# Two-layer encoder on one core: heads cross in pairs, merged rows turned in two chunks, pool products two projections later, another MLP entry

## The chip, the cores and the metric

The kernel runs on one core of one Trainium2 chip. The metric is the device time of one execution in microseconds (us), the median of several runs. TensorE (PE in the profile, PEld its weight loads) multiplies matrices, VectorE (DVE) and ScalarE (ACT) work element by element, GpSimd (POOL) does little here, and SyncE (SP) issues the DMAs. SBUF is the on-chip memory of 128 partitions, PSUM holds matmul results.

## The reference, cut to what matters

Two layers on x (1, 256, 1024), float32. Each layer is a token mixer and a gated MLP, both with RMSNorm ahead and a residual add behind.

```python
def _token_mixer(xn, w_in, w_pool, pool_scale, w_a, w_b, w_o, rel_bias):
    u, q, k, v, g_pool, g_attn = jnp.split(xn @ w_in, SPLITS, axis=-1)
    pooled = ...   # centred means of u over 2, 4, 8, 16 tokens, minus u, by 4 channel groups
    pool_out = jnp.einsum('bsgc,gcd->bsgd', pooled, w_pool).reshape(B, S, POOL_WIDTH) * pool_scale
    # 12 heads of 128 in 3 groups (window, dilation): (128,1), (512,4), (2048,16); softmax with a bias;
    # heads of the same number in the 3 groups are combined by their softmax denominators: 4 heads come out
    merged = jax.nn.sigmoid(g_pool) * (pool_out @ w_a) + jax.nn.sigmoid(g_attn) * (attn_out @ w_b)
    return merged @ w_o

def _conv_ffn(xn, w_up, conv_w, conv_b, w_down):     # D_FF = 2816 = 22 chunks of 128
    a, gval = jnp.split(xn @ w_up, 2, axis=-1)
    a = conv3(a, conv_w) + conv_b                    # depthwise along the tokens
    return (jax.nn.gelu(a) * gval) @ w_down
```

## The kernel before, in words

**Number format.** To keep float32 accuracy at TensorE's faster rate, operands are split into a high part (cast to float32r) and a low part (the difference). A product is three matmuls: high by high, high by low, low by high. Activations are split once; weights are split on the way.

**Weights.** Class `Weights` (L82 to L202) streams all weights in an order written out at L236 to L278. A raw load of 1 MB (L118, on SP's queue, three buffers `raw`) is cut into two pieces; ACT casts each to `wh` (L178) and DVE subtracts to get `wl` (L179). Five pairs wh/wl can be live, and splitting runs up to three pieces ahead of use.

**Order of a layer.** The work is written out in one stream, and a scheduler places the instructions on the engines: first values v from the normed rows; then u and the pool means; 24 projections `proj` (L491, 16 matmuls each) for q and k, in the order of `PAIRS`; then 8 pieces of `by_rows` (L589, 12 matmuls each) for the pool gate and pool_out @ w_a; 12 pieces for the attention gate and attn_out @ w_b; the output projection `residual_mm` (L518), whose last four of eight k are held back so that the first results come out early; then the MLP.

**Attention, by visits.** The last 12 projections and the 8 pieces each call `step` (L975) once: 20 visits, numbered from 0. `VISITS` (L40) gives, for heads 0 to 3, the visit of each of four functions: `scores` (L897: logits, softmax in `probs`), `turn` (L927), `parts` (L943) and `weigh` (L953). `turn` transposes the probabilities in 32 by 32 blocks on DVE (L931) into `rows`, a single buffer, and starts `cross` (L601): sixteen DMAs within SBUF of 32 partitions each (L606, on SP's queue), four per visit, that bring the blocks to their partitions in `pt`. `parts` splits the first group's probabilities into `pth` (ACT, L948) and `ptl` (DVE, L949), both from a pool tag with two buffers. `weigh` multiplies them with the values: `o_ps`, six matmuls by pth and ptl (L958) and four by pt (L962); ACT and DVE bring the result into `at2` (L967, L968).

**Pool products.** `pool_out` (L867) is a generator of four parts of twelve matmuls (L479 to L481) into `pool_ps`, split into `po` (L880, L881); one part runs after each of projections 4 to 7 (m == 1).

**Merged rows.** The gated sum must be turned for the output projection. Its first 512 channels (`way`) go through a block transpose (L1058) and `cross` under the work of the next pieces (`merged_parts`, L1036). The other 512 (`th`, `turned`, L1062 to L1072) come last and are turned by `blocks` (L609): sixteen DVE transposes (L614), each of four 32 by 32 blocks for the two token halves; then in two halves ACT casts (L1071) and DVE subtracts (L1072) into `m`.

**MLP entry.** For the first four chunks of D_FF (`ENTRY`, 512 columns of a) the projection is taken by rows (L1102 to L1129) as soon as the first tokens are normed; the rows `a_rows` are then turned by sixteen PE transposes `a_turn` (L1114) and copied by DVE (L1116) into `a_first`. `up(f)` (L1131) takes chunk by chunk: a and g projections, convolution, gelu, product; `residual_mm` for w_down follows `LAG` = 6 chunks behind.

Of the kernel before, what the change touches and what calls it, by code (L numbers as in the profile page):

```python
# [10 lines left out]
F32 = mybir.dt.float32  # L11
# [5 lines left out]
P = 128  # L17
# [19 lines left out]
WARM = (5, 1, 2, 1)  # L37
PAIRS = (2, 4, 0, 1, 3, 5)
LAG = 6
VISITS = ((0, 3, 12, 13), (1, 5, 13, 17), (6, 10, 18, 22), (7, 11, 19, 23))  # L40
ENTRY = 4
HALVES = (slice(0, 512), slice(512, D))
SEGMENTS = (HALVES, (slice(0, 512), slice(512, 768), slice(768, D)))

# [161 lines left out]
def encoder(ctx, tc, x, w_in, w_pool, pool_scale, w_a, w_b, w_o, norm1, norm2, w_up, conv_w,  # L206
# [29 lines left out]
    for l in range(DEPTH):  # L236
        for g in range(NG):
            c0 = C_V + g * 512
            slots = (("m2", 0, 2), ("m2", 1, 2), ("ybig",), ("at2",)) if g == 0 else ()
            for j in range(2):  # L240
                tag = "k1" if l == 0 and g == 1 and j == 0 else None
                W.use(rows(w_in[l], j * 512, 4, c0, 512, tag), slots[2 * j : 2 * j + 2])
        if l == 0:
            W.n_scaled = len(W.pieces)
        for c in range(3, -1, -1):
            W.use(cols(w_in[l], c * 256))
        for n, c in enumerate(PAIRS):
            pool = ([], [])
            if n == 1:
                pool = W.add(  # L250
                    w_pool[l].rearrange("g (k p) c -> p (g k) c", p=P), (8, 256),
                    [((lambda t, j=j: t[:, 4 * j : 4 * j + 4, :]), (4, 256)) for j in range(2)],
                )
                pool = (pool[:1], pool[1:])
            for j, c0 in enumerate((C_Q, C_K)):
                a, b = cols(w_in[l], c0 + c * 256)
                W.use([a] + pool[j] + [b])
        for w, c0 in ((w_in[l], C_GP), (w_a[l], 0)):
            for half in HALVES:
                for j in range(2):  # L260
                    W.use(rows(w, j * 512, 4, c0 + half.start, 512))
        for half in HALVES:
            for j in range(2):
                W.use(rows(w_in[l], j * 512, 4, C_GA + half.start, 512))
            W.use(rows(w_b[l], 0, 4, half.start, 512))
        for c in range(4):
            W.use(rows(w_o[l], c * 256))
        slots = (("v1",), ("ybig",), ("at2",))
        for j in range(2):
            W.use(rows(w_up[l], j * 512, 4, 0, 512), slots[2 * j : 2 * j + 2])  # L270
        for f in range(0, NF, 2):
            a = cols(w_up[l], f * P) if f >= ENTRY else []
            g = cols(w_up[l], DFF + f * P)
            W.use([a[0], g[0], a[1], g[1]] if a else g)
            if f >= LAG:
                W.use(rows(w_down[l], (f - LAG) * P))
        for f in range(NF - LAG, NF, 2):
            W.use(rows(w_down[l], f * P))  # L278
# [3 lines left out]
    xv = x[0].rearrange("(m t) d -> m t d", t=2)  # L282

    def gain(src):
        g = sm.tile([P, D], F32, tag="gain", bufs=1, name="gain")
        nc.sync.dma_start(out=g, in_=src.partition_broadcast(P))
        return g

# [61 lines left out]
    def load_bias():  # L350
        oh = big.tile([P, NT * 256], F32, tag="ybig", name="onehot_sb")
        nc.gpsimd.memset(oh, 0.0)
        rb = sm.tile([P, P], F32, tag="s", name="rb")
        nc.gpsimd.memset(rb, 0.0)
        for r in (0, 64):
            nc.sync.dma_start(out=oh[r : r + 33, :], in_=onehot)
            for g in range(NG):
                cc = slice(32 * g, 32 * g + HPG)
                nc.sync.dma_start(out=rb[r : r + 32, cc], in_=rel_bias[:, g * HPG : (g + 1) * HPG])
        for g in range(NG):  # L360
            nc.gpsimd.memset(rb[32:33, 32 * g : 32 * g + HPG], 1.0)
        rr = big.tile([P, P], F32R, tag="at2", name="rr")
        nc.vector.tensor_copy(rr, rb)
        nc.vector.tensor_sub(
            out=rr[64:96], in0=rb[64:96], in1=rr[64:96].bitcast(F32)
        )
        ohr = big.tile([P, NT * 256], F32R, tag="m2", name="onehot_r")
        nc.scalar.copy(out=ohr, in_=oh)
        return rr, ohr
# [239 lines left out]
    def blocks(out, in_):  # L609

        for i in range(4):
            for j in range(4):
                a, b = slice(32 * i, 32 * i + 32), slice(32 * j, 32 * j + 32)
                nc.vector.transpose(out=out[b, :, :, a], in_=in_[a, :, :, b])  # L614

    def two_parts(tag, name):

# [163 lines left out]
    for l in range(DEPTH):  # L781
# [43 lines left out]


        plh = big.tile([P, KD, 2, P], F32R, tag="ybig", name="plh")
        pll = big.tile([P, KD, 2, P], F32R, tag="xn", name="pll")
        pooled = {}
        for gi in range(3, -1, -1):  # L830
            w = WINDOWS[gi]
# [63 lines left out]
        probs, ptiles, crossing = {}, {}, []  # L895

        def scores(hh):  # L897
            probs[hh] = sm.tile([P, 2, 512], F32, tag="s", name="probs")
# [28 lines left out]

        def turn(hh):

            rows = sm.tile([P, 4, 2, 4, 32], F32, tag="gain", bufs=1, name="rows")  # L930
            nc.vector.transpose(  # L931
                out=rows.rearrange("p j t c r -> p (t c) j r"),
                in_=probs[hh].rearrange("p t (c j r) -> p (t c) j r", c=4, j=4),
            )
            if hh % 2 == 0:
                ptiles["pair"] = big.tile(
                    [P, 2, 4, 2, 4, 32], F32, tag=("ybig", "xn")[hh // 2], name="pt"
                )
            ptiles[hh] = ptiles["pair"][:, hh % 2]
            crossing.append(cross(ptiles[hh], rows))  # L940

        def parts(hh):
            pt = ptiles[hh].rearrange("p i t c r -> p c t i r")  # L943
            pth = sm.tile([P, 2, 2, P], F32R, tag="us", name="pth")
            ptl = sm.tile([P, 2, 2, P], F32R, tag="us", name="ptl")
            for c in range(2):
                hi, lo = (a[:, c].rearrange("p t (i r) -> p t i r", i=4) for a in (pth, ptl))
                nc.scalar.copy(out=hi, in_=pt[:, c])  # L948
                nc.vector.tensor_sub(out=lo, in0=pt[:, c], in1=hi.bitcast(F32))  # L949
            ptiles[hh] = pth, ptl, pt[:, 2:4]  # L950

        def weigh(hh):
            pth, ptl, pt = ptiles[hh]  # L953
            ps = acc.tile([P, 2, P], F32, tag="acc", name="o_ps")
            for kc in range(2):
                c = slice(hh * P, (hh + 1) * P)
# [16 lines left out]
                visits[visit].append((f, hh))  # L973

        def step():  # L975
            for f, hh in visits.pop(0):
                f(hh)
            if crossing and next(crossing[0], "end") == "end":
                crossing.pop(0)


        for m, c in enumerate(PAIRS):
            if m == 1:
                po2 = two_parts("m2", "po2")
                pool_parts = pool_out(po2)
            if m == 2:

                qkl = big.tile([P, 2, HPG, 2, P], F32R, tag="xn", name="qkl")
                ql, kl = qkl[:, 0], qkl[:, 1]
            for n in range(4):  # L990
                src, rest = (halves(a) for a in proj(x2))
                if m == 1:
# [52 lines left out]
        for n, cc in enumerate(HALVES):  # L1045
# [17 lines left out]
            else:  # L1063
                assert next(first, None) is None
                turned = big.tile([P, 4, 2, P], F32, tag="v0", name="turned")
                blocks(
                    turned.rearrange("p c t q -> p t c q"), th.rearrange("p t (c k) -> p t c k", c=4)
                )
                for k in range(0, 4, 2):
                    hi, lo = (a[:, 4 + k : 6 + k] for a in (mh, ml))  # L1070
                    nc.scalar.copy(out=hi, in_=turned[:, k : k + 2])  # L1071
                    nc.vector.tensor_sub(out=lo, in0=turned[:, k : k + 2], in1=hi.bitcast(F32))  # L1072
# [26 lines left out]
        acts = {}  # L1099


        a_first = big.tile([P, ENTRY, S], F32, tag="gates", name="a_first")  # L1102

        rows_of_a = big.tile([P, 2, ENTRY * P], F32, tag="m2", name="a_rows")

        def keep_entry(t, ps):
            r = rows_of_a[:, t]
            nc.scalar.copy(out=r, in_=ps)
            return r

        def turn_entry(t, r):
            pt = mmp.tile([P, ENTRY, P], F32, tag="mm", name="a_turn")
            for f in range(ENTRY):
                nc.tensor.transpose(pt[:, f, :], r[:, f * P : (f + 1) * P], ident)  # L1114
            av = a_first.rearrange("p f (m t) -> p f m t", t=2)[:, :, :, t]
            nc.vector.tensor_copy(av, pt)  # L1116

        held, ps = entry
        first = keep_entry(0, ps)
        ps = v_tile()  # L1120
        for n in range(4):
            v_sum(ps, x2, 1, n, held[n])
            if n == 1:
                turn_entry(0, first)
        for i, _ in held:
            W.free(i)
        last = keep_entry(1, ps)
        g_first = [proj(x2)]
        turn_entry(1, last)  # L1129

        def up(f):  # L1131
            w0, w1, w2, b = (prm[:, l, j * NF + f : j * NF + f + 1] for j in range(4))
            if f < ENTRY:
                a = a_first[:, f, :]
# [92 lines left out]
```

## Time and profile before

| | us |
|---|---|
| runs | 889.36, 888.7, 886.91; median 888.7 |
| profiled execution | 886.12 |
| its span | 884.3 (granted TensorE clock 0.999) |
| TensorE busy | 864.0 (98%) |
| VectorE busy | 674.0 (76%) |
| ScalarE busy | 498.2 (56%) |

The profile records one execution. Its span runs from the first to the last instruction; the rest of the execution's time, 1.8 us, lies around it. Times in a timeline count from the span's start. A line number is that of the kernel's source, but a helper has one line for all its callers, so the tile names tell them apart. A matmul's recorded duration is longer than its pitch, since matmuls overlap: 128x256 shows 0.28 us and follows at 0.12, 128x512 shows 0.39 and follows at 0.23.

### The profile page before, as it was taken

The page shows a single profiled execution, that of the slowest core. Times are in us where ns is not written, and L with a number is a line of the kernel's source. Part 1 is how long each engine was busy: PE and PEld are TensorE (multiplying, and loading weights), DVE is VectorE, ACT ScalarE, POOL GpSimd, SP SyncE. Part 2 cuts the span into 40 slices and gives each one's busy share as a digit, 9 for nine tenths or more (in the row PEclk, how much of TensorE's full clock was granted, in tenths as well). Part 3 has the DMA queues.
Part 4 walks back from the last instruction along what each step waited for, and adds up shares of the span by engine and source line. Part 5 has one row for each costly group of instructions (what it writes and reads, how often), then busy time and mean ns, then how long its engine had stood idle before and what let it go on. Part 6 is the DMA issues. An engine that isn't in the chain of part 4 may idle for free.

```text
span 884.3 us, 12329 instructions
## 1 busy us (share of the span) xinstructions
PE 864.0 (98%) x4554; PEld 739.7 (84%) x4554; DVE 674.0 (76%) x1088; ACT 498.2 (56%) x817; POOL 15.6 (2%) x45
## 2 busy tenths in 40 slices
PE   9999999999899999999999999999998999999997
PEld 7888988788788888888888898887886888888886
DVE  7997795656788987787856968774559798878774
ACT  7745554534448766666545565454444586656653
POOL 2000000000010000000000000000000100000000
PEclk9999999999999999999999999999999999999999
DMA  9668736376464565465626465455745547556541
GB/s 330 215 233 264 254 127 211 122 278 191 167 211 147 203 224 191 160 221 191 238 96 232 149 199 183 140 196 161 251 151 203 195 157 246 183 190 199 182 143 49
DMA packets 121480, 169.86 MB, mean 192 GB/s; under 512 B 5814, under 2 KB 89478, under 8 KB 121292
## 3 DMA queue, kind: packets, MB, share of 16 engines
q1 hardware_dynamic: 121404, 169.07, 57.0%
q8 instruction: 36, 0.59, 0.3%
q14 instruction: 24, 0.20, 0.1%
q10 hardware_dynamic: 16, 0.00, 0.0%
HBM read 162.74 MB, written 3.69 MB: 188 GB/s over the span
## 4 chain that ended last, share of the span: by engine, by line
PE 79%; DVE 7%; DMA 6%; SPq 5%; issue 1%; ACT 1%; POOLq 0%; DVEq 0%; ACTq 0%; POOL 0%
PE proj_ps L487 25%; PE proj_ps L489 13%; PE rows_ps L584 10%; PE v_ps L584 6%; PE res_ps L515 5%; PE res_ps L516 5%; PE res_ps L514 5%; SPq L606 5%; DMA raw<-in_w_in_dram 4%; PE v_ps L773 2%; DVE wl L179 2%; DVE turned L614 2%; PE v_ps L686 1%; ACT wh L178 1%; PE o_ps L962 1%
## 5 line engine op out<-in xcount | busy, mean ns | idle before, releaser
L179 DVE TENSOR_TENSOR wl<-raw,wh 128x1024 fp32r<-128x1024 f32 x274 | 333.8, 1223 | 143.5 <-ACT wh L178 139.3
L178 ACT CAST wh<-raw 128x1024 fp32r<-128x1024 f32 x274 | 286.5, 1050 | 213.4 <-PE proj_ps L487 69.6
L487 PE MATMUL proj_ps<-x,wh 128*128 128x512 f32 x1152 | 288.8, 392 | 0.0
L487 PEld LDWEIGHTS proj_ps<-x,wh 128*128 128x128 f32 x1152 | 208.2, 189 | 38.0
L489 PEld LDWEIGHTS proj_ps<-x,wl 128*128 128x128 f32 x1152 | 157.2, 190 | 11.3
L489 PE MATMUL proj_ps<-x,wl 128*128 128x256 f32 x1152 | 160.8, 282 | 0.0
L584 PE MATMUL rows_ps<-wh,x 128*128 128x512 f32 x256 | 81.7, 392 | 0.0
L514 PE MATMUL res_ps<-wh,actq 128*128 128x512 f32 (+1 forms) x184 | 70.2, 381 | 0.0
L515 PE MATMUL res_ps<-wl,actq 128*128 128x512 f32 (+1 forms) x184 | 70.1, 381 | 0.0
L516 PE MATMUL res_ps<-wh,actk 128*128 128x512 f32 (+1 forms) x184 | 69.9, 380 | 0.0
L584 PEld LDWEIGHTS rows_ps<-wh,x 128*128 128x128 f32 x256 | 48.1, 188 | 9.7
L584 PE MATMUL rows_ps<-wl,x 128*128 128x512 f32 x128 | 49.8, 389 | 0.0
L584 PE MATMUL rows_ps<-wh,po 128*128 128x512 f32 x128 | 40.3, 391 | 0.0
L516 PEld LDWEIGHTS res_ps<-wh,actk 128*128 128x128 f32 x184 | 34.6, 188 | 6.7
L514 PEld LDWEIGHTS res_ps<-wh,actq 128*128 128x128 f32 x184 | 34.7, 188 | 6.2
L515 PEld LDWEIGHTS res_ps<-wl,actq 128*128 128x128 f32 x184 | 34.7, 188 | 6.0
L514 PE MATMUL res_ps<-wh,m 128*128 128x512 f32 (+1 forms) x72 | 26.8, 372 | 5.6 <-ACT m L1042 5.6
L1157 ACT ACTIVATE y<-y 128x256 f32<-128x256 f32 x44 | 18.3, 416 | 24.1 <-DVE y L1154 24.0
L1140 ACT ACTIVATE y<-a,prm 128x256 f32<-128x256 f32 x36 | 21.6, 599 | 16.0 <-DVE a L510 16.0
L584 PEld LDWEIGHTS rows_ps<-wh,po 128*128 128x128 f32 x128 | 24.0, 188 | 4.9
L584 PEld LDWEIGHTS rows_ps<-wl,x 128*128 128x128 f32 x128 | 24.1, 188 | 4.7
L515 PE MATMUL res_ps<-wl,m 128*128 128x512 f32 (+1 forms) x72 | 26.8, 373 | 1.0 <-DVE wl L179 1.0
(208 smaller groups left out, 1135.2 us busy)
## 6 DMA issues: line engine op xcount, KB each, us to landing
raw<-in_w_in_dram SPq DMA_DIRECT2D x58, 1024.0 KB
raw<-in_w_up_dram SPq DMA_DIRECT2D x44, 1024.0 KB
raw<-in_w_down_dram SPq DMA_DIRECT2D x22, 1024.0 KB
raw<-in_w_a_dram SPq DMA_DIRECT2D x8, 1024.0 KB
raw<-in_w_o_dram SPq DMA_DIRECT2D x8, 1024.0 KB
pt<-rows SPq DMA_DIRECT2D x128, 32.0 KB
raw<-in_w_b_dram SPq DMA_DIRECT2D x4, 1024.0 KB
sk<-fd SPq DMA_DIRECT2D x1, 2560.0 KB
```

The lines of the kernel that those rows point to most:

```text
L178: lambda: nc.scalar.copy(out=h, in_=src),
L179: lambda: nc.vector.tensor_sub(out=l, in0=src, in1=h.bitcast(F32)),
L487: nc.tensor.matmul(ps, wh(k), x2[:, k], start=(k == 0), stop=False)
L489: nc.tensor.matmul(ps[:, 1], wl(k), x2[:, k, 0], start=False, stop=(k == nk - 1))
L514: nc.tensor.matmul(ps, ah, wh, start=first, stop=False)
L515: nc.tensor.matmul(ps, ah, wl, start=False, stop=False)
L516: nc.tensor.matmul(ps, al, wh, start=False, stop=last)
L584: nc.tensor.matmul(ps, x2[:, 2 * n + j, part, t, :], w[:, j, :], start=(n + m == 0), stop=(n == of - 1 and m == 5),)
L606: nc.sync.dma_start(out=out[b, i], in_=in_[a, j])
L614: nc.vector.transpose(out=out[b, :, :, a], in_=in_[a, :, :, b])
L1140: nc.scalar.activation(y, a, AF.Identity, bias=b, scale=w1)
L1157: nc.scalar.activation(y2, y2, AF.Tanh, scale=c)
```

## The change: what it does

1. **Pairs of heads.** Two heads' `scores` and `turn` come at neighbouring visits, write into one `rows` tile and cross together: sixteen DMAs of 32 partitions by 512 elements per pair (2 KB runs) in place of two times sixteen by 256. `parts` of the second head falls into the visit of `weigh` of the first. `step` advances the crossing before the visit's functions. The tag `gain`, which `rows` shares, doubles in size.
2. **Pool products** run after projections 6 to 9; the two weight pieces move one place back in the weights' order, the load for q of the second pair goes ahead of that of w_pool; `pll` and `rr` trade their tags `xn` and `at2`, and `po2` is allocated ahead.
3. **Merged rows in two chunks.** `blocks` becomes a generator that yields after each transpose and is called once for each half of `turned`, on two chunks of 128 channels: 32 transposes of 128 elements a partition in place of 16 of 256. The cast and subtraction of a half follow its transposes.
4. **MLP entry on the last four chunks.** Rows of a are taken for chunks 18 to 21 (`FIRST` = 18); the PE transposes and DVE copies are replaced by `blocks`, one transpose per `up(f)` of the first chunks, sixteen a layer. Chunks 0 to 17 take their own a projection; the early projection for g of chunk 0 goes.

```diff
-VISITS = ((0, 3, 12, 13), (1, 5, 13, 17), (6, 10, 18, 22), (7, 11, 19, 23))
+VISITS = ((0, 1, 12, 13), (2, 3, 14, 15), (9, 10, 21, 22), (10, 11, 22, 23))
 ENTRY = 4
+FIRST = NF - ENTRY
...
         for n, c in enumerate(PAIRS):
-            pool = ([], [])
+            q = cols(w_in[l], C_Q + c * 256)
             if n == 1:
                 pool = W.add(
...
-                pool = (pool[:1], pool[1:])
-            for j, c0 in enumerate((C_Q, C_K)):
-                a, b = cols(w_in[l], c0 + c * 256)
-                W.use([a] + pool[j] + [b])
+            k = cols(w_in[l], C_K + c * 256)
+            if n == 1:
+                k.insert(1, pool[0])
+            if n == 2:
+                q.insert(1, pool[1])
+            W.use(q + k)
...
-            W.use(rows(w_up[l], j * 512, 4, 0, 512), slots[2 * j : 2 * j + 2])
+            W.use(rows(w_up[l], j * 512, 4, FIRST * P, 512), slots[2 * j : 2 * j + 2])
         for f in range(0, NF, 2):
-            a = cols(w_up[l], f * P) if f >= ENTRY else []
+            a = cols(w_up[l], f * P) if f < FIRST else []
...
-        g = sm.tile([P, D], F32, tag="gain", bufs=1, name="gain")
+        g = sm.tile([P, 2 * D], F32, tag="gain", bufs=1, name="gain")[:, 0:D]
...
-        rr = big.tile([P, P], F32R, tag="at2", name="rr")
+        rr = big.tile([P, P], F32R, tag="xn", name="rr")
...
                 nc.vector.transpose(out=out[b, :, :, a], in_=in_[a, :, :, b])
+                yield
...
-        pll = big.tile([P, KD, 2, P], F32R, tag="xn", name="pll")
+        pll = big.tile([P, KD, 2, P], F32R, tag="at2", name="pll")
...
         def turn(hh):
-            rows = sm.tile([P, 4, 2, 4, 32], F32, tag="gain", bufs=1, name="rows")
+            pair, e = divmod(hh, 2)
+            if e == 0:
+                rows = sm.tile([P, 4, 2, 2, 4, 32], F32, tag="gain", bufs=1, name="rows")
+                pt = big.tile([P, 4, 2, 2, 4, 32], F32, tag=("ybig", "xn")[pair], name="pt")
+                ptiles[pair] = rows, pt
+            rows, pt = ptiles[pair]
             nc.vector.transpose(
-                out=rows.rearrange("p j t c r -> p (t c) j r"),
+                out=rows[:, :, e].rearrange("p j t c r -> p (t c) j r"),
                 in_=probs[hh].rearrange("p t (c j r) -> p (t c) j r", c=4, j=4),
             )
-            if hh % 2 == 0:
-                ptiles["pair"] = big.tile(
-                    [P, 2, 4, 2, 4, 32], F32, tag=("ybig", "xn")[hh // 2], name="pt"
-                )
-            ptiles[hh] = ptiles["pair"][:, hh % 2]
-            crossing.append(cross(ptiles[hh], rows))
+            if e:
+                crossing.append(cross(pt, rows))
...
         def step():
+            if crossing and next(crossing[0], "end") == "end":
+                crossing.pop(0)
             for f, hh in visits.pop(0):
                 f(hh)
-            if crossing and next(crossing[0], "end") == "end":
-                crossing.pop(0)
...
-                if m == 1:
+                if 6 <= 4 * m + n < 10:
                     next(pool_parts)
...
-                blocks(
-                    turned.rearrange("p c t q -> p t c q"), th.rearrange("p t (c k) -> p t c k", c=4)
-                )
                 for k in range(0, 4, 2):
+                    run(blocks(
+                        turned[:, k : k + 2].rearrange("p c t q -> p t c q"),
+                        th[:, :, k * P : (k + 2) * P].rearrange("p t (c k) -> p t c k", c=2),
+                    ))
                     hi, lo = (a[:, 4 + k : 6 + k] for a in (mh, ml))
...
-            if n == 1:
-                turn_entry(0, first)
+            nc.scalar.copy(out=a_rows[:, t], in_=ps)
         for i, _ in held:
             W.free(i)
-        last = keep_entry(1, ps)
-        g_first = [proj(x2)]
-        turn_entry(1, last)
+        turning = blocks(a_last.rearrange("p f (m t) -> p t f m", t=2), a_rows)
 
         def up(f):
-            if f < ENTRY:
-                a = a_first[:, f, :]
+            if f >= FIRST:
+                a = a_last[:, f - FIRST, :]
             else:
                 a = sm.tile([P, S], F32, tag="u", name="a")
                 add_up(in_order(a), [halves(b) for b in proj(x2)])
-            sums = g_first.pop() if f == 0 else proj(x2)
+                next(turning, None)
+            sums = proj(x2)
```

More of the change, by code (lines that the diff above doesn't have):

```diff
@@ L894, in encoder @@
         at2 = big.tile([P, HPG, 2, 2, P], F32R, tag="at2", name="at2")
-        probs, ptiles, crossing = {}, {}, []
+        probs, ptiles, split, crossing = {}, {}, {}, []
         def scores(hh):
@@ L928, in turn @@
         def turn(hh):
-            rows = sm.tile([P, 4, 2, 4, 32], F32, tag="gain", bufs=1, name="rows")
+            pair, e = divmod(hh, 2)
[4 more added lines that the diff above has]
+            rows, pt = ptiles[pair]
             nc.vector.transpose(
-                out=rows.rearrange("p j t c r -> p (t c) j r"),
+                out=rows[:, :, e].rearrange("p j t c r -> p (t c) j r"),
                 in_=probs[hh].rearrange("p t (c j r) -> p (t c) j r", c=4, j=4),
             )
-            if hh % 2 == 0:
-                ptiles["pair"] = big.tile(
-                    [P, 2, 4, 2, 4, 32], F32, tag=("ybig", "xn")[hh // 2], name="pt"
-                )
-            ptiles[hh] = ptiles["pair"][:, hh % 2]
-            crossing.append(cross(ptiles[hh], rows))
+            if e:
+                crossing.append(cross(pt, rows))
         def parts(hh):
-            pt = ptiles[hh].rearrange("p i t c r -> p c t i r")
+            pair, e = divmod(hh, 2)
+            pt = ptiles[pair][1][:, :, e].rearrange("p i t c r -> p c t i r")
             pth = sm.tile([P, 2, 2, P], F32R, tag="us", name="pth")
@@ L949, in parts @@
                 nc.vector.tensor_sub(out=lo, in0=pt[:, c], in1=hi.bitcast(F32))
-            ptiles[hh] = pth, ptl, pt[:, 2:4]
+            split[hh] = pth, ptl, pt[:, 2:4]
         def weigh(hh):
-            pth, ptl, pt = ptiles[hh]
+            pth, ptl, pt = split.pop(hh)
             ps = acc.tile([P, 2, P], F32, tag="acc", name="o_ps")
@@ L975, in step @@
         def step():
+            if crossing and next(crossing[0], "end") == "end":
+                crossing.pop(0)
             for f, hh in visits.pop(0):
                 f(hh)
-            if crossing and next(crossing[0], "end") == "end":
-                crossing.pop(0)
+        po2 = two_parts("m2", "po2")
+        pool_parts = pool_out(po2)
         for m, c in enumerate(PAIRS):
-            if m == 1:
-                po2 = two_parts("m2", "po2")
-                pool_parts = pool_out(po2)
             if m == 2:
@@ L991, in encoder @@
                 src, rest = (halves(a) for a in proj(x2))
-                if m == 1:
+                if 6 <= 4 * m + n < 10:
                     next(pool_parts)
@@ L1099, in encoder @@
         acts = {}
[L1102 to L1116, printed above, removed]
-        held, ps = entry
[L1119 to L1122, printed above, removed]
-            if n == 1:
-                turn_entry(0, first)
+        a_last = big.tile([P, ENTRY, S], F32, tag="gates", name="a_last")
+        a_rows = big.tile([P, 2, ENTRY, P], F32, tag="m2", name="a_rows")
+        held, ps = entry
+        for t in range(2):
+            if t:
+                ps = v_tile()
+                for n in range(4):
+                    v_sum(ps, x2, t, n, held[n])
+            nc.scalar.copy(out=a_rows[:, t], in_=ps)
         for i, _ in held:
             W.free(i)
-        last = keep_entry(1, ps)
-        g_first = [proj(x2)]
-        turn_entry(1, last)
+        turning = blocks(a_last.rearrange("p f (m t) -> p t f m", t=2), a_rows)
         def up(f):
             w0, w1, w2, b = (prm[:, l, j * NF + f : j * NF + f + 1] for j in range(4))
-            if f < ENTRY:
-                a = a_first[:, f, :]
+            if f >= FIRST:
+                a = a_last[:, f - FIRST, :]
             else:
```

## The prediction, made before the changed kernel had run

> **What bounds the kernel now.** I read the page first (busy shares, chain that ended last), then the waits of TensorE, then windows of 10 us, then timelines of the stretches that the windows mark.
>
> ```profile
> PE 864.0 (98%) x4554; PEld 739.7 (84%) x4554; DVE 674.0 (76%) x1088; ACT 498.2 (56%) x817; POOL 15.6 (2%) x45
> PE 79%; DVE 7%; DMA 6%; SPq 5%; issue 1%; ACT 1%; POOLq 0%; DVEq 0%; ACTq 0%; POOL 0%
> PE proj_ps L487 25%; PE proj_ps L489 13%; PE rows_ps L584 10%; PE v_ps L584 6%; PE res_ps L515 5%; PE res_ps L516 5%; PE res_ps L514 5%; SPq L606 5%; DMA raw<-in_w_in_dram 4%; PE v_ps L773 2%; DVE wl L179 2%; DVE turned L614 2%; PE v_ps L686 1%; ACT wh L178 1%; PE o_ps L962 1%
> ```
>
> TensorE (PE) is busy for 98% of the span of 884.3 us. Everything that the change can win is a place where PE stops, or PE work that goes. The places have names:
>
> ```profile
> PE res_ps L514 <- ACT m L1042: 5.6, 2, 2.9
> PE o_ps L958 <- DVE ptl L949: 3.7, 4, 1.7
> PE pool_ps L479 <- DVE po L881: 1.3, 1, 1.3
> PE o_ps L958 <- ACT pth L948: 1.1, 2, 0.7
> PE gain_ps L329 <- DVE ones L315: 1.0, 1, 1.0
> PE res_ps L515 <- DVE wl L179: 1.0, 4, 0.3
> ```
>
> Each row has the wait in us, the number of times and the longest. The largest, 5.6 us, is the merged rows' first crossing (`way`), whose sixteen DMAs and weight loads keep their order: not touched. The two rows of o_ps make 4.8 us in six stops, and the windows show where:
>
> ```profile
> core 0: us, PE busy (x) PEld busy (x) DVE busy (x) ACT busy (x) POOL busy (x), PEclk, DMA share, GB/s
> 140.00:150.00 10.00, 9.32 (x54) 7.58 (x53) 4.49 (x9) 3.64 (x7) 0.00 (x0) 1.00 0.93 328
> 170.00:180.00 10.00, 8.35 (x43) 6.88 (x42) 4.59 (x7) 4.88 (x8) 0.00 (x0) 1.00 0.71 227
> 580.00:590.00 10.00, 9.15 (x58) 7.99 (x59) 7.20 (x13) 4.13 (x9) 0.00 (x0) 1.00 0.53 186
> 600.00:610.00 10.00, 8.49 (x43) 6.91 (x42) 5.27 (x6) 3.81 (x6) 0.00 (x0) 1.00 0.46 144
> ```
>
> In these four windows PE lacks 0.68, 1.65, 0.85 and 1.51 us, while DVE and ACT are about half idle and PEclk is 1.00: nobody is saturated, something comes late. What is late is seen on SP, PE and DVE (times in us from the span's start, duration, and in brackets the idle time ahead with its releaser):
>
> ```profile
> 130.16 8.80 SPq L606 DMA_DIRECT2D pt<-rows  x12
> 139.06 0.52 SPq L118 DMA_DIRECT2D raw<-in_w_in_dram  x1
> ```
> ```profile
> 160.11 10.02 SPq L606 DMA_DIRECT2D pt<-rows  x16
> 170.22 0.53 SPq L118 DMA_DIRECT2D raw<-in_w_a_dram  x1
> ```
> ```profile
> 171.69 1.25 DVE L931 STREAM_TRANSPOSE rows<-probs 128x1024 f32<-128x1024 f32 x1 [2.35 <-DMA pt<-rows]
> 172.86 1.18 DVE L179 TENSOR_TENSOR wl<-raw,wh 128x1024 fp32r<-128x1024 f32 x1
> 173.97 0.75 DVE L949 TENSOR_TENSOR ptl<-pt,pth 128x256 fp32r<-128x256 f32 x2
> ```
> ```profile
> 174.44 0.38 PE L958 MATMUL o_ps<-ptl,vh 128*128 128x256 f32 x1 [1.65 <-DVE ptl L949]
> 174.66 0.28 PE L958 MATMUL o_ps<-pth,vl 128*128 128x256 f32 x1
> ```
>
> Sixteen crossing DMAs hold SP for 10.02 us, 0.63 each. At 171.69 the transpose of the next head stands at the head of DVE's queue until they land, because `rows` is one buffer; a weight split and ptl queue behind it, and PE waits for ptl. At 139.06 a raw weight load leaves SP only after twelve crossings; the pth cast queues behind that load's cast on ACT.
>
> **The change part by part.** The profiled run took 886.12 us (span plus 1.8), 2.6 under the median of 888.7; I sum against 886.12 and move the result by 2.6.
>
> *1. Two heads cross together.* Half of 128 crossing DMAs go, and inside a pair no transpose waits for a crossing. What a stop costs: its idle time, 4.8 in all, plus in each of six stops the modelled tail of the last matmul (about 0.16) and a slower restart (0.22 from 174.44 to 174.66, where the pitch is 0.12): 4.8 + 6 x 0.26 = 6.4 us. Does the pair land in time? The second head is turned at visit 3 or 15, its parts come at 9 or 21. The first pair's rows are then ready near 123; 16 issues of 0.63 with raw loads between end near 134 and land by 139, and pth is due about 142.8 (its product follows one visit ahead of where the second head's stands now, 146.2). The second pair: ready about 164, issued 174.6, landed 176, pth due about 179.4. These places are estimates, with 3 to 4 us in hand. So the six stops go: **-6.4**.
>
> The new order has a wait of its own. pth and ptl of a head fill both buffers of their pool; the second head's parts now follow the first's directly, on ACT and DVE, and wait there until PE has read the first's.
>
> ```profile
> L948 ACT CAST pth<-pt x16: 394/402/408, 128.9 to 622.6; 128x256 fp32r<-128x256 f32 x16
> L949 DVE TENSOR_TENSOR ptl<-pt,pth x16: 384/417/420, 130.1 to 623.9; 128x256 fp32r<-128x256 f32 x16
> ```
>
> From the start of the matmul that frees pth: 0.28 to its end, 0.05 to ACT, 0.40 cast, 0.05, 0.42 subtraction: 1.2 us until the second head's first ptl is there. PE covers the free matmul, one more and four of pt by v (6 x 0.12 = 0.71) and its first product; the rest, about 0.5, is idle. Four pairs: **+2.0** (0 if other work is in between, 6.4 if the whole chain of 1.6, two subtractions long, is bare in each pair).
>
> *2. Merged rows by two chunks.* 32 transposes of 128 elements take the place of 16 of 256, on DVE, in a stretch where DVE is already what PE waits for.
>
> ```profile
> L614 DVE STREAM_TRANSPOSE turned<-th x32: 424/435/441, 236.1 to 677.2; 32x256 f32<-32x256 f32 x32
> L931 DVE STREAM_TRANSPOSE rows<-probs x8: 1226/1240/1246, 116.1 to 605.9; 128x1024 f32<-128x1024 f32 x8
> ```
> ```profile
> 236.12 7.17 DVE L614 STREAM_TRANSPOSE turned<-th 32x256 f32<-32x256 f32 x16
> 243.31 2.36 DVE L179 TENSOR_TENSOR wl<-raw,wh 128x1024 fp32r<-128x1024 f32 x2
> 245.59 1.29 DVE L1072 TENSOR_TENSOR m<-turned,m 128x512 fp32r<-128x512 f32 x2
> 246.79 2.35 DVE L179 TENSOR_TENSOR wl<-raw,wh 128x1024 fp32r<-128x1024 f32 x2
> ```
> ```profile
> 246.21 0.39 PE L515 MATMUL res_ps<-wl,m 128*128 128x512 f32 x1
> 248.07 0.50 PE L515 MATMUL res_ps<-wl,m 128*128 128x512 f32 x1 [0.31 <-DVE wl L179]
> 249.21 0.50 PE L515 MATMUL res_ps<-wl,m 128*128 128x512 f32 x1 [0.17 <-DVE wl L179]
> ```
>
> Half a transpose isn't in the trace. 435 ns at 256 and 1240 at 1024 elements a partition give 1.05 ns an element and 167 ns fixed, so 128 elements take 301; with the gap of 13 (7.17 / 16 = 448, less 435) 316 ns. Bounds: 224 (half of 448) and 448 (nothing saved). I take 316, on the line of the same operation. 32 x 0.316 = 10.1 us against 7.17. In the changed order one m subtraction (0.6) comes inside, then the four wl with one m between: the wl of held pieces 4 to 7 are ready at 248.0, 249.1, 250.9 and 252.1. PE wants the first at 246.21: it stops 1.85, then about 0.4, 0.8, and some tenths in restarts, 3.4 together, where it loses 1.04 now (the waits of res_ps L515, halved per layer, with tails). Raw loads that wait for these wl leave about 3.5 us later, and the MLP's first norm shifts by about as much as PE itself. **+2.4 a layer, +4.8**; 0 at 224 ns (transposes end as now), +13 at 448.
>
> [...]
>
> *3. MLP entry on the last four chunks.* Sixteen PE transposes go.
>
> ```profile
> 268.13 0.60 PE L1114 MATMUL a_turn<-ident,a_rows 128*128 128x128 f32 x4
> 268.48 1.64 PE L584 MATMUL v_ps<-at,x 128*128 128x512 f32 x6
> ```
>
> Four occupy 0.35 us of issue: 4 x 0.35 = **-1.4**. DVE gains 32 transposes like L614's (14.3 us) for four copies, spread over the first half of the MLP; no row of the waits above lies there, so PE's queue of split weights covers them. Without that cover, 14 us would be the limit. The other moves (which chunk takes its own projection first) leave the number of matmuls the same.
>
> *4. Pool products two projections later.*
>
> ```profile
> 80.39 2.00 PE L487 MATMUL proj_ps<-x,wh 128*128 128x512 f32 x8
> 83.19 0.28 PE L479 MATMUL pool_ps<-plh,wh 128*128 128x256 f32 x1
> 85.38 0.38 PE L479 MATMUL pool_ps<-plh,wh 128*128 128x256 f32 x1 [1.31 <-DVE po L881]
> ```
> ```profile
> 81.48 2.00 ACT L178 CAST wh<-raw 128x1024 fp32r<-128x1024 f32 x2 [1.95 <-DMA raw<-in_w_in_dram]
> ```
>
> The stop of 1.6 (with tail and restart) goes. But the raw load behind it still lands at 81.4. A projection takes 2.8 (80.39 to 83.19), and without the 12 pool matmuls of 0.12 ahead of it the one at 80.39 starts at 78.95; the next piece is then wanted at 81.74 and cast at 82.53. A stop of 0.8 stays: **-0.8** (from -1.6 to +2). The second layer shows no such row: 0.
>
> Sum: -6.4 + 2.0 + 4.8 - 1.4 - 0.8 = **-1.8**: 884.3 as the profiled run is counted, **886.9** against the median, -0.2%.
>
> **The rivals**, as medians.
>
> *Half transposes cost half.* Then part 2 is free: 886.9 - 4.8 = 882.1. For it: the elements are the same. Against: two sizes on one line with 167 ns fixed. [...]
>
> *The pair's own chain takes the gain back* (slower side). ACT and DVE are in order: while the second head's casts wait for buffers, weight casts and splits queue behind them. If the 1.6 us of each pair is bare, part 1 is worth 0: -1.4 - 0.8 + 4.8 = +2.6, 891.3. It decides from where PE has nothing between the two heads; by the changed order only four short matmuls lie there.
>
> *Half transposes cost as much as whole ones* (slower): 886.9 + 8.4 = 895.3.
>
> *The crossing doesn't come in time.* If a 64 KB DMA holds SP twice as long, 20 us instead of 10, each pair lands 3 to 5 us late: about 901. Against: the issue of a 1 MB raw load takes 0.53.
>
> **How the numbers follow.** A measurement of this kernel tells about 0.3% (2.7 us) from no change. Forecast 0.46 (885 to 889: faster 0.21, same 0.25); cheap halves 0.14 (faster); chain in the pair 0.22 (same 0.08, slower 0.14); full-price halves 0.10 (slower); late crossing 0.06 (slower); 0.02 for a larger gain. Faster 0.37, same 0.33, slower 0.30. The range runs from 881.0 (cheap halves, with the 1 us that pool may add) to 895.5 (full-price halves); late crossings and the rest, under 0.1, are left out.
>
> **What would show it.** Right: no wait of o_ps above 0.5 at the first head of a pair, and short ones at the second; L617 for turned at 0.30 each; the wait of res_ps for wl growing from 1.0 to about 5 in all; no a_turn; the way stop of 5.6 as it was. Wrong: ptl or rows still released by a pt DMA; waits of v_ps or proj_ps in the first half of the MLP; half transposes at 0.22 or 0.44.

## The result, and the profile after

| | before | changed |
|---|---|---|
| median of 10 runs, first chip, us | 889.13 (886.91 to 889.8) | 883.38 (882.01 to 885.64) |
| ratio, 95% interval | | 0.9943 (0.993 to 0.9955) |
| ratio on a second chip (run e6_after), 95% interval | | 0.9963 (0.9951 to 0.9975) |
| profiled execution, us; its span; granted clock | 886.12; 884.3; 0.999 | 885.41; 883.6; 0.994 |

Faster by 0.4 to 0.6%: by the ratios 5.1 us on the first chip and 3.3 on the second (the medians differ by 5.8 and 3.9), where 1.8 was forecast. The two profiled executions differ by only 0.7 us. They aren't alike: that of before has a granted clock of 0.999, which one of its 18 runs on the next chip had too (886.0 us); the other 17 stand at 0.991 to 0.997 and take 885.9 to 890.5. More on that below.

The page of the changed kernel, busy shares and the chain that ended last:

```profile
PE 864.5 (98%) x4538; PEld 740.3 (84%) x4538; DVE 689.0 (78%) x1148; ACT 496.1 (56%) x817; POOL 17.3 (2%) x45
PE 87%; DVE 5%; DMA 4%; SPq 2%; ACT 1%; issue 1%; POOL 0%; POOLq 0%; ACTq 0%
```

PE has 16 instructions fewer and DVE 60 more. SP's part of the chain falls from 5% to 2% and PE's rises from 79% to 87%: crossings seldom set any more when PE can go on. The waits of TensorE in the changed kernel (waited for: us, times, longest):

```profile
PE res_ps L517 <- ACT m L1047: 5.2, 2, 2.6
PE res_ps L518 <- DVE wl L180: 3.7, 6, 1.9
PE proj_ps L490 <- ACT wh L179: 1.8, 1, 1.8
PE gain_ps L332 <- DVE ones L318: 1.0, 1, 1.0
PE v_ps L587 <- DVE x L462: 0.8, 2, 0.4
PE v_ps L690 <- ACT xuh L646: 0.2, 1, 0.2
```

Against the list of before: both rows of o_ps are gone (4.8 us). The wait for wl has grown from 1.0 to 3.7, a wait of v_ps for x is new (0.8), and the stop at pool_ps (1.3) has become one at proj_ps (1.8). The way stop is where it was (5.6, now 5.2). DVE's own waits for the crossings (rows <- DMA pt<-rows, 6.6 us in four before) are gone as well, which agrees with the crossings as what held up ptl and pth.

**The pair lands in time.** SP in the changed kernel, first pair of the first layer:

```profile
125.02 2.48 SPq L609 DMA_DIRECT2D pt<-rows  x4
127.61 0.52 SPq L119 DMA_DIRECT2D raw<-in_w_in_dram  x1
128.17 6.27 SPq L609 DMA_DIRECT2D pt<-rows  x8
134.54 0.89 SPq L119 DMA_DIRECT2D raw<-in_w_in_dram  x1
135.48 2.41 SPq L609 DMA_DIRECT2D pt<-rows  x4
```

An issue of 64 KB takes 0.62 us (2.48 / 4), as one of 32 KB did (10.02 / 16): twice the bytes hold SP no longer. The last leaves at 137.9, and the cast of pth starts at 145.11, held by nothing from the crossing. PE and ACT there:

```profile
147.98 0.28 PE L964 MATMUL o_ps<-pth,vl 128*128 128x256 f32 x1
148.10 1.05 PE L968 MATMUL o_ps<-pt,v 128*128 128x128 f32 x8
148.91 0.36 PE L964 MATMUL o_ps<-pth,vh 128*128 128x256 f32 x1
149.11 0.38 PE L964 MATMUL o_ps<-ptl,vh 128*128 128x256 f32 x1
```
```profile
145.11 0.70 ACT L954 CAST pth<-pt 128x256 fp32r<-128x256 f32 x2
148.18 0.71 ACT L954 CAST pth<-pt 128x256 fp32r<-128x256 f32 x2 [2.37 <-PE o_ps L964]
```

The second head's cast does wait for its buffer, 2.37 us, but ACT has time: PE meanwhile runs eight matmuls of pt by v, and goes on at 148.91 with no idle time in brackets.

**The merged rows.** DVE in the changed kernel, first layer, and PE in the second:

```profile
234.79 6.32 DVE L617 STREAM_TRANSPOSE turned<-th 32x128 f32<-32x128 f32 x20
241.12 0.69 DVE L1078 TENSOR_TENSOR m<-turned,m 128x512 fp32r<-128x512 f32 x1
241.83 3.79 DVE L617 STREAM_TRANSPOSE turned<-th 32x128 f32<-32x128 f32 x12
245.65 2.36 DVE L180 TENSOR_TENSOR wl<-raw,wh 128x1024 fp32r<-128x1024 f32 x2
247.93 0.68 DVE L1078 TENSOR_TENSOR m<-turned,m 128x512 fp32r<-128x512 f32 x1
248.53 2.35 DVE L180 TENSOR_TENSOR wl<-raw,wh 128x1024 fp32r<-128x1024 f32 x2
```
```profile
677.00 0.39 PE L517 MATMUL res_ps<-wh,m 128*128 128x512 f32 x1
679.33 0.50 PE L518 MATMUL res_ps<-wl,m 128*128 128x512 f32 x1 [1.94 <-DVE wl L180]
680.46 0.50 PE L518 MATMUL res_ps<-wl,m 128*128 128x512 f32 x1 [0.17 <-DVE wl L180]
682.20 0.50 PE L518 MATMUL res_ps<-wl,m 128*128 128x512 f32 x1 [0.52 <-DVE wl L180]
```

The 32 transposes take 6.32 + 3.79 = 10.1 us where 16 took 7.17, and the splits of wl for the held pieces follow that much later. PE loses 2.10 + 0.34 + 0.69 = 3.1 us in the second layer (start to start beyond the pitch). The first layer shows only 1.5: PE had just run for 3.4 us at half clock (from 234.25 to 237.66), so it came to the wait late.

**The clock.** Windows of the changed kernel (columns as before; PEclk is the granted clock):

```profile
80.00:84.00 4.00, 2.25 (x14) 1.87 (x13) 0.36 (x2) 1.41 (x2) 0.00 (x0) 1.00 0.89 307
84.00:88.00 4.00, 4.00 (x15) 3.29 (x14) 4.00 (x5) 3.70 (x5) 0.00 (x0) 0.57 0.04 13
230.00:234.00 4.00, 1.36 (x7) 0.82 (x6) 3.41 (x6) 2.02 (x3) 0.00 (x0) 1.00 1.02 391
234.00:238.00 4.00, 4.00 (x12) 3.14 (x11) 3.86 (x13) 0.07 (x1) 0.00 (x0) 0.57 0.72 278
```

A stop stands in the first and third window, a stretch at little over half clock in the window behind it. The profiled run of before had no such stretch.

### The profile page after: what moved, and what is told of

The parts are those of the page before. It is cut to its first block, busy times and chain, and to the rows that moved or that the text cites. A ratio compares the mean times of both kernels' runs of the same rounds, so it can differ in the third digit from the quotient of the medians.

```text
span 883.6 us, 12221 instructions
## 1 busy us (share of the span) xinstructions
PE 864.5 (98%) x4538; PEld 740.3 (84%) x4538; DVE 689.0 (78%) x1148; ACT 496.1 (56%) x817; POOL 17.3 (2%) x45
## 3 DMA queue, kind: packets, MB, share of 16 engines
HBM read 162.74 MB, written 3.69 MB: 188 GB/s over the span
## 4 chain that ended last, share of the span: by engine, by line
PE 87%; DVE 5%; DMA 4%; SPq 2%; ACT 1%; issue 1%; POOL 0%; POOLq 0%; ACTq 0%
PE proj_ps L490 28%; PE rows_ps L587 15%; PE proj_ps L492 14%; PE v_ps L587 6%; PE res_ps L518 5%; PE res_ps L517 5%; PE res_ps L519 5%; PE v_ps L777 2%; DVE turned L617 2%; DMA sk<-fd 2%; PE v_ps L690 1%; DMA raw<-in_w_up_dram 1%; DVE wl L180 1%; SPq L609 1%; PE o_ps L968 1%; PE s_ps L911 1%
```

## The experiments

Ratios are to the kernel before on the same chip. The first four were timed together (before: 887.96 us, median of 18), the next four on another chip (887.51, of 20), the last two later (888.11, of 17). The changed kernel itself stands at 0.9943 and 0.9963.

**Merged rows in one go.**

```diff
-                for k in range(0, 4, 2):
-                    run(blocks(turned[:, k : k + 2]..., th[:, :, k * P : (k + 2) * P]...))
+                run(blocks(turned..., th...))
+                for k in range(0, 4, 2):
```

> The changed kernel with the merged rows turned in one go again (16 transposes of 256 elements, as before). Theory (each part is worth its PE stops): the waits of res_ps for wl fall from 3.7 us to 1.0 and those of v_ps for x (0.8) go, so 2 to 4 us faster than the changed kernel: 880 against 883.4. Rival (the split rows pay for themselves because the first half's cast starts earlier): the same or slower than 883.4.

Measured: 877.98 us, 0.9885 (0.9869 to 0.9901). Against the changed kernel's ratios that is 5.2 and 6.9 us faster, more than expected. Three of its waits of TensorE and its transposes:

```profile
PE res_ps L517 <- ACT m L1047: 5.2, 2, 2.8
PE proj_ps L490 <- ACT wh L179: 0.9, 1, 0.9
PE res_ps L518 <- DVE wl L180: 0.5, 2, 0.3
```
```profile
231.99 7.17 DVE L617 STREAM_TRANSPOSE turned<-th 32x256 f32<-32x256 f32 x16
```

The wait for wl is 0.5 in place of 3.7, and that of v_ps for x is gone. So the two chunks cost time, and this kernel beats both the one before and the changed one.

**Every head crosses by itself again.**

```diff
-VISITS = ((0, 1, 12, 13), (2, 3, 14, 15), (9, 10, 21, 22), (10, 11, 22, 23))
+VISITS = ((0, 3, 12, 13), (1, 5, 13, 17), (6, 10, 18, 22), (7, 11, 19, 23))
+        # turn, parts, weigh, step as in the kernel before
```

> The changed kernel with every head crossing by itself again, at the visits of before. Theory: the six stops of o_ps come back, 5.8 to 6.4 us: about 889.5. Rival (the pair's own chain on ACT and DVE takes part of the gain back): 886 or less.

Measured: 891.73 us, 1.0042 (1.0029 to 1.0055): 7.0 and 8.8 us slower than the changed kernel, and slower than before. That is more than the expected 5.8 to 6.4. The waits come back:

```profile
PE o_ps L962 <- DVE ptl L953: 4.1, 5, 1.6
PE o_ps L962 <- ACT pth L952: 0.7, 2, 0.4
```

The rival fell: nothing of the gain was taken back.

**The MLP entry of before.** Edit: the entry's code, its weight columns and the order of a and g as in the kernel before.

> The changed kernel with the MLP entry of before (chunks 0 to 3, PE transposes). Theory: sixteen PE transposes come back, 1.4 us: about 884.8. Rival (32 transposes more on DVE in the changed kernel cost something in the MLP): the same as the changed kernel or faster.

Measured: 885.68 us, 0.9973 (0.9956 to 0.9991): 0.9 to 2.7 us slower than the changed kernel, with intervals that touch. That agrees with 1.4. The trace has no wait of proj_ps or res_ps in the MLP in either kernel, so the 32 transposes on DVE are covered.

**The pool products of before.** Edit: projections 4 to 7 and the weight order of before.

> The changed kernel with the pool products after projections 4 to 7 and the weight order of before. Prediction's step: 0.8 us slower than the changed kernel. Theory from the two traces (a stop of 1.5 at pool_ps was traded for one of 1.9 at proj_ps): 0.4 us faster, within the noise.

Measured: 884.19 us, 0.9954 (0.9937 to 0.9971), between the two ratios of the changed kernel: no difference that this can tell. Its trace has a stop of 2.2 us at pool_ps. Over all traces the stop at pool_ps was 1.5, 3.2 and 2.2 with the old order, and with the new one the stop at proj_ps went from none (e2) to 2.0 (e7 aside, where the loads ahead of it were moved). A stop that hangs on the landing of a raw load varies by more than the move is worth.

**The kernel before once more.** Edit: none.

> The kernel before once more, for a second trace on another chip. Theory (the first trace, at a granted clock of 0.999, was an undisturbed one): this trace may hold stretches of about 3 us at half clock behind long stops, each losing 1.2 to 2.6 us; the stages from attention to the MLP keep 193, 36.4 and 172 us otherwise. Rival (stages vary by more than that from run to run without any drop of the clock): a stage differs by over 1 us with the clock full.

Measured: 887.49 us, 1.0008 (0.9993 to 1.0024). The profiled span is 889.5, 5.2 over the first. The windows around one o_ps stop and around one way stop of this second trace:

```profile
172.00:178.00 6.00, 4.36 (x21) 3.41 (x20) 3.59 (x5) 2.75 (x5) 0.00 (x0) 1.00 0.61 199
178.00:184.00 6.00, 6.00 (x27) 5.01 (x26) 1.56 (x2) 1.74 (x3) 0.00 (x0) 0.72 0.72 225
234.00:240.00 6.00, 3.42 (x16) 2.52 (x15) 4.46 (x7) 3.12 (x4) 0.00 (x0) 1.00 0.95 333
240.00:244.00 4.00, 4.00 (x13) 3.08 (x12) 3.90 (x10) 0.02 (x1) 0.00 (x0) 0.58 0.79 308
```

Four stretches at half clock lose about 1.3, 1.3, 1.6 and 1.7 us by their pitch, 5.9 together, and the stop at pool_ps is 1.8 longer than in the first trace. About 1.1 behind each way stop doesn't lengthen its stage (36.9 against 36.4): it hides the waits for wl. That leaves about 5.5 for the 5.2 between the spans. So the clock makes the larger part of the difference between the two traces of before, as expected. The pool stop, which the expectation hadn't named, is the second cause, and there the rival held: 1.8 us more with the clock full.

**The changed kernel once more.** Edit: none.

> The changed kernel once more, beside the kernel without the two chunks on the same chip. Theory: 0.994 of the kernel before; the stage of the merged rows takes 39.0 to 39.4 us where it took 36.4, a half-clock stretch ahead of the waits for wl being hidden by them. Rival: with the clock full the stage is under 38.

Measured: 883.62 us, 0.9963 (0.9951 to 0.9975). From the first res_ps to the MLP's first proj_ps this trace takes 39.0 and 39.6 us in the two layers, the first one 39.0 and 39.4, that of before 36.4 and 36.4. In this trace the half-clock stretches ahead of the waits for wl lose about 1.6 us each, the waits shrink from 3.1 to 1.5, and the stage keeps its length: hidden, as expected. The rival fell with the trace of e3, which has the clock full there, the entry of before, and 39.5 and 39.4 us.

**Bias loads off SP's queue.** On top of the merged rows in one go:

```diff
-            nc.sync.dma_start(out=bt[:, :, blk * P : (blk + 1) * P], in_=src)
+            nc.gpsimd.dma_start(out=bt[:, :, blk * P : (blk + 1) * P], in_=src)
```

> The changed kernel with the merged rows turned in one go, and the five loads of the bias table moved from SP's queue to POOL's. Theory (the stop of 1.1 to 1.9 us at the first projection of the second pair stands because the raw load there leaves SP behind these five issues): the raw load leaves 4 to 5 us earlier, the stop goes, about 1 us faster than without the move: 877. Rival (the load waits for its buffer or for bandwidth): the stop stays, 878.

Measured: 878.62 us, 0.9904 (0.9889 to 0.992): no gain. The raw loads left at 69.1 where they had left at 75.1, but the stop only moved one projection on:

```profile
PE res_ps L517 <- ACT m L1047: 5.4, 2, 2.9
PE proj_ps L490 <- DVE q L1015: 1.9, 1, 1.9
```

Now DVE, with weight splits queued that had all come at once, is late with q. The load that left 6 us earlier came only 1.4 us earlier: the cast that waits for it starts at 80.18, against 81.53 without the move. The DMA engines were busy all the while (DMA share 0.96 from 69 to 75 and 1.05 from 75 to 80.2), so this is the rival's bandwidth. The stretch lacks split weights, and an earlier issue doesn't bring them.

**Half of the merged rows' crossing on POOL's queue.** On top of the merged rows in one go: in `cross` for `way`, the DMAs with odd j go to POOL.

> The changed kernel with the merged rows turned in one go, and every other DMA of the merged rows' crossing issued on POOL's queue. Theory (SP's 16 issues of 0.6 us set when the first merged rows arrive): the crossing ends up to 5 us earlier, the two stops of res_ps for m (5.2 us) go, and with them half-clock stretches: 872 to 874. Rival (an issue on POOL's queue takes longer, or landing lags): 878 or more.

Measured: 877.85 us, 0.9894 (0.988 to 0.9908): no gain, against an expectation of 4 to 6 us. Its waits of res_ps:

```profile
PE res_ps L517 <- ACT m L1076: 3.5, 2, 2.1
PE res_ps L519 <- DVE m L1077: 0.9, 2, 0.5
```

The stop for the first rows (L1047) did go, so SP's issues set it: in the first layer they took 3.69 + 1.15 us on SP and 4.16 on POOL, where e1 has 7.48 + 2.41 on SP. PE then came to the turned rows (L1076, L1077) before DVE had made them, and waited there. Merged rows have two ends that come almost together.

**Without the products of pt by v.**

```diff
-            for g in (1, 2):
-                hd = (g - 1) * HPG + hh
-                for t in range(2):
-                    nc.tensor.matmul(ps[:, t, :], v[:, t, hd * P : (hd + 1) * P], pt[:, g - 1, t, :], ...)
```

> The changed kernel with the four products of pt by v per head left out, so the second and third group's attention isn't computed. They show as eight matmul records of 0.11 us. Theory (these eight cover the wait of the second head's pth and ptl for their buffers): without them waits of o_ps for pth and ptl stand at the second head of each pair, about 0.6 for pth and 0.3 for ptl by the page's durations, 2 to 4 us in four pairs, where the changed kernel has none; the matmuls left out are worth about 7 us, so 876 to 880. Rival (the wait is covered by other work, or the buffers come free sooner): no wait of o_ps at all.

Measured: 877.29 us, a single run. Its waits of TensorE, all of them:

```profile
PE res_ps L517 <- ACT m L1040: 6.6, 2, 4.0
PE res_ps L518 <- DVE wl L180: 2.0, 6, 0.5
PE gain_ps L332 <- DVE ones L318: 1.0, 1, 1.0
PE v_ps L587 <- DVE x L462: 0.8, 2, 0.4
PE v_ps L690 <- ACT xuh L646: 0.2, 1, 0.2
```

The theory fell: no wait of o_ps, though the time lies in its 876 to 880. In this trace two matmuls of rows_ps stand between the heads and three of s_ps behind the second head's first product: with less cover, the order of PE's work had become another. The buffer wait is covered here by other ready work put between, so not by these eight matmuls in particular.

**MLP entry and pool products alone.** Edit: merged rows in one go and every head by itself, both as above.

> Only the MLP entry and the pool products changed against the kernel before; merged rows in one go, every head crossing by itself. Theory (parts add up): 1.4 us for the PE transposes and about 0.5 for the pool stop under the kernel before, so 0.997 to 0.998 of it; and the pair crossing alone, against the kernel with merged rows in one go (0.9885), is worth 7 to 8 us. Rival (pair crossing and two chunks only pay together): below 0.993.

Measured: 886.53 us, 0.9981 (0.9967 to 0.9995), a hair above the expected 0.997 to 0.998, which its interval covers. Against merged rows in one go with pairs (0.9885) the pair crossing is worth 0.0096 of 888, 8.5 us, give or take about 2 by the two intervals; 7 to 8 was expected. Parts add up within that.

## Why the prediction was right or wrong

Faster was the likeliest of three, with 0.37; the range held the time. The size came out two to three times the forecast, because one gain was put too low. That faster came first was in part luck: 0.14 of its 0.37 stood on half transposes that cost half, which the runs rule out, and without them same would have led, 0.33 to 0.23. Two misses also partly cancel in the sum: the pairs brought about 3 to 4 us more than counted, the two chunks cost 0.5 to 2 us more. In us, beside what the runs show:

| step | predicted | shown |
|---|---|---|
| 1. six o_ps stops go | -6.4 | gone in every trace with pairs |
| 1. new wait inside the pair | +2.0 | 0 |
| 1. together | -4.4 | -7.0 to -8.8 (e2), -8.5 (e10 against e1) |
| 2. two chunks | +4.8 | +5.2 and +6.9 (e1), +5.4 (e2 against e10) |
| 3. MLP entry | -1.4 | -0.9 to -2.7 (e3) |
| 4. pool products | -0.8 | nothing measurable (e4) |

**Step 1, the stops:** right, in cause and place. The crossing leaves SP at 137.9 (134 was estimated) and pth follows at 145.1 (142.8).

**Step 1, the pair's own chain:** this is the step that failed. "PE covers the free matmul, one more and four of pt by v (6 x 0.12 = 0.71)": the trace of before had 64 of these matmuls over eight heads, so eight per head and not four, and the second head's product starts without idle time.

```profile
L962 PE MATMUL o_ps<-pt,v x64: 272/275/348, 132.1 to 626.0; 128*128 128x128 f32 x64
```

The chain itself was sized well: from the matmul that frees pth (147.98) to the first with the new ptl (149.11) it takes 1.13 us, and 1.2 was computed. What was too short is the cover. The deeper fault is to price a wait from a fixed neighbourhood: e9 shows that other work is put there when it lacks. The rival that built on the same chain falls with it.

**Step 1, the rest of the gain.** Pairs brought 8.5 us where 6.4 and the six stops were counted. In the traces of e10 and e1, from the first q projection to the first res_ps, the layers take 193.9 and 191.8 us against 189.3 and 187.5; of the 4.6 and 4.3, about 0.5 in the first layer is a shorter proj_ps stop. The trace with single heads has seven stops of o_ps, not six, 6.3 us start to start, with about 0.1 for each restart. The remaining 1 to 1.5 us aren't pinned to one row. Half-clock stretches behind o_ps stops, as at 178 to 184 above, can lengthen some runs; these two traces have none there.

**Step 2:** right in mechanism and in the price of a half transpose. It took 303 ns, the median in this row of the changed kernel (least, median and longest in ns), and 301 was drawn from the line:

```profile
L617 DVE STREAM_TRANSPOSE turned<-th x64: 292/303/308, 234.8 to 677.7; 32x128 f32<-32x128 f32 x64
```

The 32 take 10.1 us, as computed (301 and a gap of 13 make 314, not 316, which changes nothing here). So both rivals on its price, 224 and 448, are out. The wl splits came as computed: PE loses 3.1 a layer to them where the clock is full, 3.4 was computed, and the wait for wl, forecast at about 5 in all, is 5.2 in e3 and 3.7 in the first trace, whose first layer hides part of it. What was too small is "the MLP's first norm shifts by about as much as PE itself": v_ps waits for x in both layers, 0.4 each in the list, 0.53 and 0.57 start to start, new in the changed kernel and gone in e1. The prediction had named waits of v_ps in the MLP as a sign of being wrong. In all it is 3.0 to 3.5 a layer instead of 2.4, by the stage with the clock full: 39.4 in e3, with the entry of before, against 36.4 in the kernel before, and 39.4 in the changed kernel's second layer against 35.9 in e1's first.

**Step 3:** agrees with the computed 1.4, within a wide interval; DVE's 14 us (32 transposes of 436 ns, a_last<-a_rows in the changed kernel's trace) are covered.

**Step 4:** the stop that stays was given 0.8 and is 1.8 in the first trace. The load behind it left SP at 75.58, after five bias loads, and landed at 82.5, with the DMA engines fully busy from 75 to 82 (share 1.02); 81.4 was taken from the trace of before. With a landing that varies by microseconds, the sign couldn't be told.

**The baseline.** I took 2.6 us from profiled run to median as a constant. The runs show that it isn't. Of 67 runs of before on three chips, the three with a clock of 0.999 took 886.0, 886.0 and 887.3 us, and the first profiled run was of this kind. The 21 at 0.997 took 886.8 in the mean, the 18 at 0.992 and 0.993 took 888.3, the seven at 0.991 took 889.9 (those between fall out of step: 886.5 at 0.994, 889.0 at 0.995 and 0.996). The changed kernel hides part of the same loss under its waits for wl. The trace of e3 has a clock of 0.999 and spans 883.9; less 1.4 for its entry, an undisturbed changed kernel would span 882.5 against 884.3, which is the 1.8 on record, while the ratios make 3.3 to 5.1. The run of e3 at 0.999 took 885.7, its four at 0.994 and 0.995 took 884.2 to 885.9, and its two at 0.993 took 888.2 and 888.6: in four of six a lower clock cost nothing. That this is the whole of the gap is argued, not shown: no trace of the changed kernel itself with a clock of 0.999 was taken.

## What to carry to other kernels

Look for what releases a wait: here sixteen small DMAs per head held SP's queue for 10 us, and DMAs of twice the size were issued in the same 0.62 us each, so half as many were enough. Before splitting a block of work on an engine that the next stage already waits for, price the fixed part per instruction; here about 170 ns for each of 16 more transposes a layer (two of 303 ns for one of 435) came straight out of the end, and undoing it gives 0.9885 in place of 0.994 to 0.996. A stop that is removed may uncover the next one close behind it (e7, e8), so look for the second-latest arrival before promising the whole stop.

## What the runs showed of the hardware

In ten of the twelve traces TensorE's granted clock fell to half behind stops: matmuls of 512 columns then follow at 0.43 us in place of 0.23 (in the changed kernel's trace from 84.06 and from 234.25, for 3.41 us each), for 3.41 us in 19 of 22 stretches and for 6.83 in three. In the twelve traces, 21 of 35 stops of 1.8 us or more (start to start beyond the pitch) had such a stretch within 2.3 us of their end, against 1 of 8 stops of 1.4 to 1.75; two traces (before and e3, both with a clock of 0.999) had none at all behind stops of up to 3.0.

In these traces a stop with a stretch and one without differ mostly in where they fall on a fixed beat. The stretches of one trace start whole multiples of 3.413 us apart: in the second trace of before at 87.03, 179.19, 240.63 and 674.12, that is 27, 18 and 127 beats, in the changed kernel's at 84.06 and 234.25, 44 beats. A trace without stretches has its beat from the moments at which the clock rises at its start and falls behind its last matmuls (before: 5.47, where matmuls of 128 columns go from a pitch of 0.21 to one of 0.11 us, and 882.69, 257 beats). Here are the windows of this beat around the second layer's way stop (columns as before), first from the second trace of before, where the stop is 3.1 us, then from the first, where it is 3.0:

```profile
670.71:674.12 3.41, 0.51 (x3) 0.18 (x2) 2.56 (x5) 1.90 (x3) 0.00 (x0) 1.00 1.02 386
674.12:677.54 3.42, 3.42 (x9) 2.67 (x10) 3.35 (x8) 0.28 (x1) 0.00 (x0) 0.50 0.82 320
```
```profile
664.24:667.65 3.41, 2.19 (x10) 1.50 (x8) 2.81 (x4) 0.76 (x2) 0.00 (x0) 1.00 0.99 376
667.65:671.07 3.42, 1.77 (x8) 1.48 (x9) 2.60 (x6) 1.99 (x3) 0.00 (x0) 1.00 1.02 406
671.07:674.48 3.41, 3.41 (x17) 2.83 (x16) 3.31 (x8) 1.05 (x1) 0.00 (x0) 1.00 0.40 149
```

The one stop lies within a window and leaves PE 0.51 us of work in it; the other is split over two, with 2.19 and 1.77. Over the twelve traces, from about 20 to 866 us, all 17 windows of the beat with PE busy for 1.31 us or less were followed by half clock, 5 of 11 with 1.48 to 1.77, and of those above none that ran at full clock itself (three at half clock already were, which makes the 6.83). In the changed kernel's trace the windows with 0.78 (230.83 to 234.25) and 1.66 (80.65 to 84.06) were followed by half clock, that with 1.75 (664.32 to 667.74) was not. So a stop of about 3 us cost up to 1.7 us more (the second layer's in the second trace of before) or nothing (the same in the first), by its place on the beat, and the beat lies differently in these three traces: it has a mark at 83.97 in the first of before, at 83.62 in the second and at 84.06 in the changed kernel's. Why the 11 in between differ stays open.
